# Attention's values for two heads at once in plain fp32, v kept in fp32, key norms spread by transposes

## The chip, the cores and the metric

The kernel runs on one core of one Trainium2 chip. The metric is the device time of one execution in microseconds (us), the median of several runs. In the profile PE is TensorE (products), PEld its weight loads, DVE VectorE, ACT ScalarE, POOL GpSimd, and SP the engine that issues most DMAs.

## What is computed

One layer of a hybrid decoder, for a new prompt of 1024 tokens and for 64 sample tokens (8 sequences of 8) that continue from caches. The width is 1024.

```python
h = rmsnorm(x); proj = h @ w_in                    # 1024 -> 3328
o_rw = rwkv7(proj[:, :1024])                       # 4 heads of 64, keys normed per head
o_cv = short_conv(proj[:, 1024:1792])              # gated convolution, 3 taps
q, k, v = proj[:, 1792:]                           # 8 heads of 64
q, k = rmsnorm(q), rmsnorm(k)                      # per head
z = (q @ k.T) / 8 + bias                           # stick-breaking attention
beta, keep = sigmoid(z), sigmoid(-z)               # masked: keys before the query
wts = beta * (product of keep over later keys)
o_sb = wts @ v
x = x + concat(o_rw, o_cv, o_sb) @ w_out
x = x + relu(rmsnorm(x) @ w_up)**2 @ w_down        # 4096 wide
x = x + sigmoid(rmsnorm(x) @ w_ple_gate) * (p @ w_ple_proj)
```

In the RWKV part the keys kk = k * k_k are divided by their norm over each head's 64 channels. The new k and v rows are outputs too. Everything is fp32.

## The kernel before

**Precision.** Most products are made of fp32r operands: an fp32 value is split into a high part (a copy to fp32r, on ACT) and a low part (the difference, on DVE or POOL), and a product is the sum of high by high, low by high and high by low, three fp32r products into one PSUM bank. Smaller products of the recurrence, the decode step and the transposes are plain fp32.

**Order.** The kernel is traced as one program in which the stages follow each other; a planner then simulates the engines and writes out the order of each engine and of each DMA queue, from what is ready and what was traced first. So products of later stages stand between those of earlier ones wherever they are ready. A few places fix the order by hand (`issue_after`, `high_priority`, `keep_in_program_order`). `run` steps several generators in turn. Tiles come from pools with a fixed number of buffers; a new tile waits until the last use of the buffer that it takes.

**Key norms (L400 to L434).** For each of two groups j of 128 channels, `rw_tile` projects kx, L410 sums the squares per head with tokens on the partitions, and L412/L413 make 1 / sqrt (`rk`, 128 tokens x 9 blocks x 2 heads). The norms must then be spread over the 64 channels and turned so that channels lie on the partitions: L422 writes the broadcast high part in fp32r, L425 the low part, and L431 multiplies each of 9 blocks of both parts with an fp32r identity (18 products for each j). L433 multiplies kx with the result. After it come the matrices of the recurrence (`wkv_products`), and for j = 1 `wkv_base`, a chain of small DVE steps, whose result goes out to DRAM and comes back for the recurrence.

**Projections (L890 to L918).** v is projected first, then q and k, in blocks of 128 tokens; `project` copies a block from PSUM to `nat`. For v (n == 2) it writes the output and splits the block (L866 on ACT, L867 on POOL) into `spl`, which holds for four heads 64 high and 64 low columns; L868 writes it to `v_s` in DRAM, 16 writes. `stack` transposes q and k, splits them and writes `stk_s`.

**Attention (L923 to L1016).** `attention` is traced twice: for the first 512 queries (q0, q1 = 0, 2), with the convolution stepping beside it (`run(*[conv] * 5, *[att] * 4)`), and for the last 512 (2, 4), ahead of the MLP. A unit is a head h and a block qb of 256 queries, head by head; 16 units in each call. `prep` loads a head's stacked keys and queries and its values `vs` (high and low columns side by side). `weights` makes, for each half of the block (128 queries i), the scores by L961 and L962, the sigmoids on ACT, the masks on POOL (L968), the scan over later keys (L970) and the product with beta (L972) on DVE, or on POOL for odd i in the second call. `values` follows AHEAD = 2 units later. It takes the keys 256 at a time: four transposes (L990) of 128 x 128 weights into one of two banks, the high part by ACT and the low part by DVE (`split`, L60 and L61), then for each 128 keys a product of `vs` with the high part (L1000) and one with the low part (L1001), both 128 columns wide since `vs` holds high and low, into one output bank (`obank`, a single bank). L1003 copies one half of the output, L1004 adds the other, and L1005 writes 64 rows to `mix_s` from SP.

**Convolution (L1023 to L1082).** Three groups of 256 columns of w_in; the last (L1068) is loaded as one set of weights and used for j = 0 and 1.

Of the kernel before, what the change touches and what calls it, by code (L numbers as in the profile page):

```python
# [21 lines left out]
F32 = mybir.dt.float32  # L22
F32R = mybir.dt.float32r
# [8 lines left out]
NP = 1024  # L32
# [3 lines left out]
T = NP + NS  # L36
# [5 lines left out]
NA = 15  # L42
AA = 2
CA = (5, 4)
AB_ = 2


@with_exitstack
def hybrid_step(ctx: ExitStack, tc: tile.TileContext, I, O):
# [6 lines left out]
    def f(t):  # L56
        return t.bitcast(F32)

    def split(dst_hi, dst_lo, src):
        S.copy(dst_hi, src)  # L60
        V.tensor_sub(dst_lo, src, f(dst_hi))  # L61

# [28 lines left out]
    stk_s = dram.tile([2, 8, 2, 64, NP], F32, name="stk_s")  # L91
    v_s = dram.tile([8, 8, 128, 128], F32, name="v_s")
    new_s = [dram.tile([NS, 512], F32, name=f"new{n}") for n in range(3)]
# [27 lines left out]
    make_identity(nc, ident)  # L121
    ident_r = consts.tile([128, 128], F32R)
    G.tensor_copy(ident_r, ident)
    bones = consts.tile([128, 128], F32)
# [275 lines left out]
    for j in range(2):  # L400
# [12 lines left out]
        V.reciprocal(rk, rk)  # L413
        rbs = []
        for a in range(2):
            rb = pe_tile("rb", F32R)
            rbs.append((rb, rp.tile([128, 2, 64], F32R, name=f"rb8{a}")))
            for d, i0, i1 in ((rb[:, :1024], 0, 8), (rbs[a][1].rearrange("p s d -> p (s d)"), 8, 9)):
                d = d.rearrange("p (i s d) -> p i s d", i=i1 - i0, s=2)
                src = rk[:, i0:i1, :, None].to_broadcast([128, i1 - i0, 2, 64])  # L420
                if a == 0:
                    V.tensor_copy(d, src)  # L422
                else:
                    h = rbs[0][0][:, :1024] if i0 == 0 else rbs[0][1].rearrange("p s d -> p (s d)")
                    V.tensor_sub(d, src, f(h).rearrange("p (i s d) -> p i s d", i=i1 - i0, s=2))  # L425
        for t0, n in CH:
            ps = tr()
            for t in range(t0, t0 + n, 128):
                r = min(128, T - t)
                for a in range(2):  # L430
                    PE.matmul(ps[:, t - t0:t - t0 + r], rbs[a][0][:, t:t + 128] if t < NP else rbs[a][1].rearrange("p s d -> p (s d)"),  # L431
                              ident_r[:, 128 - r:], start=a == 0, stop=a == 1)
            V.scalar_tensor_tensor(kn[:, t0:t0 + n], kx[:, t0:t0 + n], P1("k_k", j), ps[:, :n], op0=ALU.mult,  # L433
                                   op1=ALU.mult)  # L434
# [414 lines left out]
    def project(n, ps, i0, nat, i):  # L849

        t0 = 128 * (i0 + i)
        flat = nat[:, i]
        S.copy(flat, ps)
        if n < 2:
            normed(flat, ps)
        to = outs[n][0][0, 0].rearrange("t h d -> t (h d)") if n else None
        if n == 1:
            SP.dma_start(to[t0:t0 + 128, :], gained(n, flat))
        if n == 2 and i:
            SP.dma_start(to[t0 - 128:t0 + 128, :].rearrange("(i p) c -> p i c", p=128), nat)  # L860
        if n == 2:
            src = flat.rearrange("p (h d) -> p h d", h=8)
            for hf in range(2):
                hs = slice(4 * hf, 4 * hf + 4)
                spl = sbp.tile([128, 4, 128], F32R, name="spl", tag="st", bufs=4)
                S.copy(spl[:, :, 0:64], src[:, hs])  # L866
                G.tensor_sub(spl[:, :, 64:128], src[:, hs], f(spl[:, :, 0:64]))  # L867
                SP.dma_start(v_s[hs, i0 + i].rearrange("h p e -> p h e"), f(spl))  # L868

    def stack(hf, n, i0, nat):  # L870
# [12 lines left out]
        for e in range(2):  # L883
            for s in range(2):
                (S, SP)[e].dma_start(stk_s[n, 4 * hf + s:4 * hf + 4:2, e, :, i0 * 128:i0 * 128 + 256]
                                     .rearrange("r d t -> d r t"),
                                     f(hl[e])[64 * s:64 * s + 64])

# [34 lines left out]
    def attention(ap, q0, q1, zbank, wbank, obank, AHEAD):  # L923
# [5 lines left out]

        heads = {}  # L930

        def prep(h):

            stk = []
            for name, n, r0 in (("k", 1, 0), ("q", 0, 256 * q0), ("x", 0, 256 * q0)):
                r = slice(r0, 256 * q1)
                o = ap.tile([128, 256 * q1 - r0], F32R, name=f"stk_{name}", bufs=2)
                if name == "x":
                    for e in range(2):
                        SP.dma_start(f(o)[64 * e:64 * e + 64], stk_s[n, h, 1 - e, :, r])  # L940
                else:
                    SP.dma_start(f(o), stk_s[n, h, :, :, r].rearrange("e d t -> (e d) t"))
# [5 lines left out]
        wts = {}  # L948

        def weights(h, qb):  # L950
            kk, qa, qx, _ = heads[h]
            for i in (2 * qb, 2 * qb + 1):
                L = 128 * (i + 1)
                q = slice(i * 128 - 256 * q0, i * 128 + 128 - 256 * q0)
                beta = ap.tile([128, 256 * q1], F32, name="beta", bufs=2 * AHEAD + 2)
                keep = ap.tile([128, 256 * q1 + 1], F32, name="keep", bufs=3 if q0 else 2)
# [15 lines left out]
                (G if i % 2 and q0 else V).tensor_mul(beta[:, 0:L], beta[:, 0:L], keep[:, 1:L + 1])  # L972
                wts[h, i] = beta

        def values(h, qb):
            vs = heads[h][3]
            pr, s = divmod(h, 2)
            d = slice(64 * s, 64 * s + 64)
            po = obank()
            last_kt = 2 * qb + 1  # L980
            for g in range(qb + 1):
                pw = wbank()
                wh = ap.tile([128, 2, 256], F32R, name="wth", bufs=2)
                wl = ap.tile([128, 2, 256], F32R, name="wtl", bufs=2)
                p3 = pw.rearrange("p (k q) -> p k q", k=2)
                for e in range(2):
                    kt = 2 * g + e
                    for i in range(2):
                        if 2 * qb + i >= kt:
                            PE.transpose(p3[:, e, i * 128:i * 128 + 128],  # L990
                                         wts[h, 2 * qb + i][:, kt * 128:kt * 128 + 128], ident)
                if g < qb:
                    split(wh, wl, p3)
                else:
                    split(wh[:, 0], wl[:, 0], p3[:, 0])
                    split(wh[:, 1, 128:], wl[:, 1, 128:], p3[:, 1, 128:])
                for e in range(2):
                    kt = 2 * g + e
                    c = slice(128 if kt == last_kt else 0, 256)
                    PE.matmul(po[:, c], vs[:, kt, :], wh[:, e, c], start=kt == 0, stop=False)  # L1000
                    PE.matmul(po[:, c], vs[:, kt, :], wl[:, e, c], start=False, stop=kt == last_kt)  # L1001
            o32 = ap.tile([128, 256], F32, name="o32", bufs=2)
            S.copy(o32[d], po[64 - 64 * s:128 - 64 * s, 0:256])  # L1003
            V.tensor_add(o32[d], po[d, 0:256], o32[d])  # L1004
# [3 lines left out]
        prep(0)  # L1008
        for n in range(len(units) + AHEAD):
            if n < len(units):  # L1010
                if n % (q1 - q0) == 0 and units[n][0] < 7:
                    prep(units[n][0] + 1)
                weights(*units[n])
            if n >= AHEAD:
                values(*units[n - AHEAD])
            yield  # L1016
# [6 lines left out]
    def convolution():  # L1023
        cst = cv.tile([16, 256], F32, name="cst")
        SP.dma_start(cst, I["state_conv"][0].rearrange("b i c -> (b i) c"))
        CV0 = 1024
# [11 lines left out]
        for j in range(2):  # L1038
# [17 lines left out]
            for i in range(2):  # L1056
# [10 lines left out]
                                   op0=ALU.mult, op1=ALU.add)  # L1067
        w = W.load(w_in[:, CV0:CV0 + 256])  # L1068
        for j in range(2):
            y = cc[j]  # L1070
            for t0, n in CH:
                ps = gemm_cv()
                gemm_t(ps, w, j, hT, t0, n)
                np_ = min(n, NP - t0)
                V.tensor_mul(y[:, t0:t0 + np_], ps[:, :np_], y[:, t0:t0 + np_])
                if np_ < n:
                    y3 = ue[j][:, 0:NS].rearrange("p (b j) -> p b j", j=NJ)
                    V.tensor_mul(y3, ps[:, np_:n].rearrange("p (b j) -> p b j", j=NJ),
                                 y[:, NP + 2:NP + 2 + NB * 10].rearrange("p (b j) -> p b j", j=10)[:, :, 0:NJ])
                yield  # L1080
# [607 lines left out]
```

## Time and profile before

| | us |
|---|---|
| median of 3 runs | 1682.45 (1681.75 to 1683.1) |
| the profiled execution | 1685.16 |
| its span from first to last instruction | 1683.5 |

The profile is one execution. Its page gives the busy time of each engine, the chain of work that ended last, and groups of instructions by line; other views give busy time by stage, each engine's waits by who ended them, and single instructions in order of time. Engines work beside each other, so idle time of one that the others do not wait for costs nothing. The starts of PE's products are good, their ends are modelled: the cost of a product is read from its start to the next start.

The mean granted clock of PE is 0.986 over the span. Stages lie at about these times: key norms 88 to 140 us, projection of v from 165 us, first attention call with the convolution from about 455 us, second call until about 866 us with products of the output projection and the MLP beside it, then the decode step and the rest of the MLP.

### The profile page before, as it was taken

The page shows a single profiled execution, that of the slowest core. Times are in us where ns is not written, and L with a number is a line of the kernel's source. Part 1 is how long each engine was busy: PE and PEld are TensorE (multiplying, and loading weights), DVE is VectorE, ACT ScalarE, POOL GpSimd, SP SyncE. Part 2 cuts the span into 40 slices and gives each one's busy share as a digit, 9 for nine tenths or more (in the row PEclk, how much of TensorE's full clock was granted, in tenths as well). Part 3 has the DMA queues.
Part 4 walks back from the last instruction along what each step waited for, and adds up shares of the span by engine and source line. Part 5 has one row for each costly group of instructions (what it writes and reads, how often), then busy time and mean ns, then how long its engine had stood idle before and what let it go on. Part 6 is the DMA issues. An engine that isn't in the chain of part 4 may idle for free.

```text
span 1683.5 us, 29402 instructions
## 1 busy us (share of the span) xinstructions
PE 1627.7 (97%) x11229; PEld 1435.7 (85%) x11229; DVE 1052.4 (63%) x1822; ACT 791.9 (47%) x1583; POOL 716.8 (43%) x799
## 2 busy tenths in 40 slices
PE   5999999999998999999999999999999999999998
PEld 5999777778897777888887778988999999999898
DVE  5366834455389679878754345277777776768432
ACT  6733235334256467666543444374444444437321
POOL 5221412133255454433435644367555545638210
PEclk8999999999999999999999999999999999999999
DMA  6134575444445453443245556322222232322211
GB/s 206 65 119 138 159 184 135 108 111 120 115 130 175 146 156 105 129 128 106 80 140 167 175 160 213 92 76 89 87 90 89 86 92 88 98 76 88 72 46 41
DMA packets 201470, 196.93 MB, mean 117 GB/s; under 512 B 57969, under 2 KB 161425, under 8 KB 201202
## 3 DMA queue, kind: packets, MB, share of 16 engines
q1 hardware_dynamic: 189330, 173.52, 34.6%
q0 software_dynamic: 5120, 16.78, 3.2%
q10 hardware_dynamic: 6880, 4.75, 1.2%
q8 instruction: 88, 1.44, 0.4%
q14 instruction: 52, 0.43, 0.1%
HBM read 158.03 MB, written 36.98 MB: 116 GB/s over the span
## 4 chain that ended last, share of the span: by engine, by line
PE 49%; DVE 4%; DMA 3%; ACT 1%; issue 1%; POOL 1%; ACTq 0%; DVEq 0%; POOLq 0%; SPq 0%
PE b L1144 11%; PE b L1145 11%; PE b L1146 11%; PE b L1501 3%; PE b L1502 3%; PE b L1503 3%; DMA wr<-in_w_up 1%; PE b L990 1%; PE b L1269 1%; DMA wr<-in_w_down 1%; PE b L1001 1%; PE b L1000 1%; DMA kpg<-in_cache_k,idx 1%; DVE x L1541 1%; PE b L1250 1%
## 5 line engine op out<-in xcount | busy, mean ns | idle before, releaser
L1125 POOL TENSOR_TENSOR wl<-wr,wh 128x512 fp32r<-128x512 f32 x137 | 198.0, 1450 | 207.7 <-ACT wh L1124 190.8
L1541 DVE TENSOR_TENSOR x<-b,x 128x288 f32<-128x288 f32 (+1 forms) x384 | 198.3, 528 | 86.7 <-PE b L1146 85.6
L1124 ACT CAST wh<-wr 128x512 fp32r<-128x512 f32 x233 | 143.8, 622 | 220.6 <-PE b L1145 153.4
L1144 PE MATMUL b<-ah,wh 128*128 128x288 f32 (+1 forms) x612 | 202.2, 331 | 2.5 <-DVE x L1541 1.4
L1146 PE MATMUL b<-ah,wl 128*128 128x288 f32 (+1 forms) x612 | 200.7, 328 | 0.0
L1145 PE MATMUL b<-al,wh 128*128 128x288 f32 (+1 forms) x612 | 200.7, 328 | 0.0
L1144 PE MATMUL b<-nh,wh 128*128 128x512 f32 (+1 forms) x352 | 131.5, 374 | 5.7 <-DVE x L1456 2.1
L1145 PE MATMUL b<-nl,wh 128*128 128x512 f32 (+1 forms) x352 | 130.4, 370 | 0.0
L1146 PE MATMUL b<-nh,wl 128*128 128x512 f32 (+1 forms) x352 | 130.0, 370 | 0.0
L1144 PEld LDWEIGHTS b<-ah,wh 128*128 128x128 f32 x612 | 114.8, 188 | 13.1 <-DVE x L1541 3.9
L1145 PEld LDWEIGHTS b<-al,wh 128*128 128x128 f32 x612 | 115.0, 188 | 8.2 <-issue 0.8
L1146 PEld LDWEIGHTS b<-ah,wl 128*128 128x128 f32 x612 | 114.9, 188 | 8.0
L173 PE MATMUL b<-h_hi,wh 128*128 128x384 f32 (+1 forms) x336 | 114.7, 341 | 1.3 <-ACT xs L353 0.6
L174 PE MATMUL b<-h_lo,wh 128*128 128x384 f32 (+1 forms) x336 | 113.8, 339 | 0.0
L175 PE MATMUL b<-h_hi,wl 128*128 128x384 f32 (+1 forms) x336 | 112.3, 334 | 0.0
L970 DVE TENSOR_TENSOR_SCAN keep<-keep,onesq 128x128 f32<-128x128 f32 (+3 forms) x64 | 98.5, 1539 | 16.7 <-POOL keep L968 16.1
L161 POOL TENSOR_TENSOR wl<-wr,wh 128x512 fp32r<-128x512 f32 x40 | 54.9, 1387 | 103.4 <-ACT wh L158 102.5
L1125 POOL TENSOR_TENSOR wsl<-s,wsh 128x512 fp32r<-128x512 f32 x60 | 79.0, 1337 | 35.9 <-ACT wsh L1124 29.0
L1125 DVE TENSOR_TENSOR wl<-wr,wh 128x512 fp32r<-128x512 f32 x96 | 75.5, 789 | 25.3 <-ACT wh L1124 21.8
L1144 PEld LDWEIGHTS b<-nh,wh 128*128 128x128 f32 x352 | 66.4, 189 | 17.4 <-DVE x L1456 2.5
L908 PE MATMUL b<-wl,h_hi 128*128 128x512 f32 x192 | 77.7, 405 | 1.8 <-DVE wl L161 1.8
L908 PE MATMUL b<-wh,h_hi 128*128 128x512 f32 x192 | 78.5, 411 | 0.0
(471 smaller groups left out, 4655.2 us busy)
## 6 DMA issues: line engine op xcount, KB each, us to landing
wr<-in_w_up SPq DMA_DIRECT2D x64, 512.0 KB
wr<-in_w_down SPq DMA_DIRECT2D x64, 512.0 KB
wr<-in_w_in SPq DMA_DIRECT2D x26, 512.0 KB
wr<-in_w_out SPq DMA_DIRECT2D x16, 512.0 KB
xt<-in_x_prompt SPq DMA_DIRECT2D x8, 512.0 KB
v_s<-spl SPq DMA_DIRECT2D x16, 256.0 KB
stk_s<-sth ACTq DMA_DIRECT2D x32, 128.0 KB
stk_s<-stl SPq DMA_DIRECT2D x32, 128.0 KB
```

What stands on the lines that cost most here:

```text
L161: sub[k0 // step % 2].tensor_sub(lo, raw[:, c:c + 512], f(hi))
L173: PE.matmul(ps[:, :n], wh[k][:, c], a, start=(k == 0), stop=False)
L174: PE.matmul(ps[:, :n], wh[k][:, c], b, start=False, stop=False)
L175: PE.matmul(ps[:, :n], wl[k][:, c], a, start=False, stop=(k == nk - 1))
L908: last = PE.matmul(ps[i], x[:, t0:t0 + 128], wt, start=start, stop=stop)
L970: V.tensor_tensor_scan(keep[:, 0:L][:, ::-1], keep[:, 0:L][:, ::-1], onesq[:, 0:1].to_broadcast([128, L]), 1.0, op0=ALU.mult, op1=ALU.mult)
L1124: S.copy(h3, src)
L1125: (sub or G).tensor_sub(l3, src, f(h3))
L1144: PE.matmul(ps[:, :n], w(0, k, m), a, start=(k == 0), stop=False)
L1145: PE.matmul(ps[:, :n], w(0, k, m), b, start=False, stop=False)
L1146: PE.matmul(ps[:, :n], w(1, k, m), a, start=False, stop=(k == nk - 1))
L1541: V.tensor_add(p.x[:, m, t0:t0 + n], ps[:, :n], p.x[:, m, t0:t0 + n])
```

## The change

- `values` takes a pair of heads. For every 128 keys both heads' weights are transposed into one bank (`p3`, heads by queries), one ACT copy brings them to SBUF in fp32 (`wt`), and two plain fp32 products follow, one for each head, with 64 columns of `vs` each, into the upper and the lower 64 partitions of the output bank. There is no split and no second product. One ACT copy takes both heads' output, and the DMA to `mix_s` is issued from ACT.
- The values are called when the second head of a pair has its weights. AHEAD is 1 in both calls. `beta` has its own buffers for even and odd i, 3 + AHEAD of each (before, 2 * AHEAD + 2 for both), those of even i 128 columns shorter.
- `v_s` holds v in fp32, by token block, written from `nat` with four DMAs; `vs` is loaded once for a pair, with one buffer in the second call and two in the first.
- The key norms are broadcast once in fp32 (`rb`, `rb8`) and turned by nine plain transposes for each j. `ident_r` goes.
- The last convolution weights are loaded as two sets of 128 columns, the second after the products of j = 0.

```diff
-AA = 2
+AA = 1
-AB_ = 2
+AB_ = 1
...
-        rbs = []
-        for a in range(2):
-            rb = pe_tile("rb", F32R)
...
+        rb = pe_tile("rb")
+        rb8 = rp.tile([128, 2, 64], F32, name="rb8")
+        for d, i0, i1 in ((rb[:, :1024], 0, 8), (rb8.rearrange("p s d -> p (s d)"), 8, 9)):
+            V.tensor_copy(d.rearrange("p (i s d) -> p i s d", i=i1 - i0, s=2),
+                          rk[:, i0:i1, :, None].to_broadcast([128, i1 - i0, 2, 64]))
         for t0, n in CH:
             ps = tr()
-            for t in range(t0, t0 + n, 128):
-                r = min(128, T - t)
-                for a in range(2):
-                    PE.matmul(ps[:, t - t0:t - t0 + r], rbs[a][0][:, t:t + 128] if t < NP else ...,
-                              ident_r[:, 128 - r:], start=a == 0, stop=a == 1)
+            for t in range(t0, min(t0 + n, NP), 128):
+                PE.transpose(ps[:, t - t0:t - t0 + 128], rb[:, t:t + 128], ident)
+            if t0 + n == T:
+                PE.transpose(ps[:, n - 128:n], rb8.rearrange("p s d -> p (s d)"), ident)
...
         if n == 2 and i:
             SP.dma_start(to[t0 - 128:t0 + 128, :].rearrange("(i p) c -> p i c", p=128), nat)
-        if n == 2:
-            src = flat.rearrange("p (h d) -> p h d", h=8)
-            for hf in range(2):
-                hs = slice(4 * hf, 4 * hf + 4)
-                spl = sbp.tile([128, 4, 128], F32R, name="spl", tag="st", bufs=4)
-                S.copy(spl[:, :, 0:64], src[:, hs])
-                G.tensor_sub(spl[:, :, 64:128], src[:, hs], f(spl[:, :, 0:64]))
-                SP.dma_start(v_s[hs, i0 + i].rearrange("h p e -> p h e"), f(spl))
+            SP.dma_start(v_s[i0:i0 + 2].rearrange("i p c -> p i c"), nat)
...
-            vs = ap.tile([128, 2 * q1, 128], F32R, name="vs", bufs=2)
-            SP.dma_start(f(vs), v_s[h, 0:2 * q1].rearrange("i p e -> p i e"))
-            heads[h] = stk + [vs]
+            heads[h] = stk
+            if s == 0:
+                vals[pr] = ap.tile([128, 2 * q1, 128], F32, name="vs", bufs=1 if q0 else 2)
+                SP.dma_start(vals[pr], v_s[0:2 * q1, :, 128 * pr:128 * pr + 128].rearrange("i p c -> p i c"))
...
-                beta = ap.tile([128, 256 * q1], F32, name="beta", bufs=2 * AHEAD + 2)
+                beta = ap.tile([128, 256 * q1 - 128 + 128 * (i % 2)], F32, name=f"beta{i % 2}", bufs=3 + AHEAD)
...
+        def values(pr, qb, wts):
+            vs = vals[pr]
             po = obank()
             last_kt = 2 * qb + 1
+            for kt in range(last_kt + 1):
+                p3 = wbank().rearrange("p (s q) -> p s q", s=2)
+                i0 = kt == last_kt
+                c = slice(128 * i0, 256)
+                for s in range(2):
+                    for i in range(i0, 2):
+                        PE.transpose(p3[:, s, i * 128:i * 128 + 128], wts[s][i][:, kt * 128:kt * 128 + 128], ident)
+                w = ap.tile([128, 2, 256], F32, name="wt", bufs=3)
+                S.copy(w[:, :, c], p3[:, :, c])
+                for s in range(2):
+                    PE.matmul(po[hs(s), c], vs[:, kt, hs(s)], w[:, s, c], start=kt == 0, stop=kt == last_kt)
             o32 = ap.tile([128, 256], F32, name="o32", bufs=2)
-            S.copy(o32[d], po[64 - 64 * s:128 - 64 * s, 0:256])
-            V.tensor_add(o32[d], po[d, 0:256], o32[d])
-            SP.dma_start(mix_s[4 + pr, d, qb * 256:qb * 256 + 256], o32[d])
+            S.copy(o32, po[:, 0:256])
+            S.dma_start(mix_s[4 + pr, :, qb * 256:qb * 256 + 256], o32)
...
+            h, qb = units[n - AHEAD] if n >= AHEAD else (0, 0)
+            if h % 2:
+                values(h // 2, qb, [made.pop((h - 1 + s, qb)) for s in range(2)])
...
-        w = W.load(w_in[:, CV0:CV0 + 256])
         for j in range(2):
+            w = W.load(w_in[:, CV0 + 128 * j:CV0 + 128 * j + 128], ncol=128)
...
-                gemm_t(ps, w, j, hT, t0, n)
+                gemm_t(ps, w, 0, hT, t0, n)
```

More of the change, by code (lines that the diff above doesn't have):

```diff
@@ L91, in hybrid_step @@
     stk_s = dram.tile([2, 8, 2, 64, NP], F32, name="stk_s")
-    v_s = dram.tile([8, 8, 128, 128], F32, name="v_s")
+    v_s = dram.tile([8, 128, 512], F32, name="v_s")
     new_s = [dram.tile([NS, 512], F32, name=f"new{n}") for n in range(3)]
@@ L121, in hybrid_step @@
     make_identity(nc, ident)
-    ident_r = consts.tile([128, 128], F32R)
-    G.tensor_copy(ident_r, ident)
     bones = consts.tile([128, 128], F32)
@@ L928, in attention @@
         V.tensor_scalar(bias[:, 1], bias[:, 0], -1.0, None, op0=ALU.mult)
-        heads = {}
+        heads, vals = {}, {}
         def prep(h):
+            pr, s = divmod(h, 2)
             stk = []
             for name, n, r0 in (("k", 1, 0), ("q", 0, 256 * q0), ("x", 0, 256 * q0)):
-                r = slice(r0, 256 * q1)
+                src = stk_s[n, h, :, :, r0:256 * q1]
                 o = ap.tile([128, 256 * q1 - r0], F32R, name=f"stk_{name}", bufs=2)
@@ L939, in prep, with hs @@
                     for e in range(2):
-                        SP.dma_start(f(o)[64 * e:64 * e + 64], stk_s[n, h, 1 - e, :, r])
+                        SP.dma_start(f(o)[64 * e:64 * e + 64], src[1 - e])
                 else:
-                    SP.dma_start(f(o), stk_s[n, h, :, :, r].rearrange("e d t -> (e d) t"))
+                    SP.dma_start(f(o), src.rearrange("e d t -> (e d) t"))
                 stk.append(o)
-            vs = ap.tile([128, 2 * q1, 128], F32R, name="vs", bufs=2)
-            SP.dma_start(f(vs), v_s[h, 0:2 * q1].rearrange("i p e -> p i e"))
-            heads[h] = stk + [vs]
-        wts = {}
+            heads[h] = stk
+            if s == 0:
+                vals[pr] = ap.tile([128, 2 * q1, 128], F32, name="vs", bufs=1 if q0 else 2)
+                SP.dma_start(vals[pr], v_s[0:2 * q1, :, 128 * pr:128 * pr + 128].rearrange("i p c -> p i c"))
+        def hs(s):
+            return slice(64 * s, 64 * s + 64)
         def weights(h, qb):
-            kk, qa, qx, _ = heads[h]
+            kk, qa, qx = heads[h]
+            wts = []
             for i in (2 * qb, 2 * qb + 1):
@@ L972, in weights @@
                 (G if i % 2 and q0 else V).tensor_mul(beta[:, 0:L], beta[:, 0:L], keep[:, 1:L + 1])
[L973 to L978, printed above, removed]
+                wts.append(beta)
+            return wts
+        def values(pr, qb, wts):
+            vs = vals[pr]
             po = obank()
             last_kt = 2 * qb + 1
[L981 to L1001, printed above, removed]
@@ L1010, in attention @@
             if n < len(units):
[L1011 to L1015, printed above, removed]
+                h, qb = units[n]
+                if qb == q0 and h < 7:
+                    prep(h + 1)
+                made[h, qb] = weights(h, qb)
+            h, qb = units[n - AHEAD] if n >= AHEAD else (0, 0)
+            if h % 2:
+                values(h // 2, qb, [made.pop((h - 1 + s, qb)) for s in range(2)])
```

17 lines of the change are left out of this document (2 added, 15 removed).

## The prediction

> **What bounds the kernel now.** I read the page's engine totals first, then the busy time by stage, then the waits of TensorE (PE), then single instructions in order of time.
>
> ```profile
> span 1683.5 us, 29402 instructions
> PE 1627.7 (97%) x11229; PEld 1435.7 (85%) x11229; DVE 1052.4 (63%) x1822; ACT 791.9 (47%) x1583; POOL 716.8 (43%) x799
> ```
>
> PE is busy 97% of the span, so what counts is PE's own time and the few places where it waits. The change sits in three stages: key norms (88 to 140 us), the projection of v (165 to 250) and attention (440 to 870). Each row gives length, then busy time and instructions of PE, PEld (weight loads), DVE, ACT and POOL, then granted clock, DMA share and GB/s.
>
> ```profile
> core 0: us, PE busy (x) PEld busy (x) DVE busy (x) ACT busy (x) POOL busy (x), PEclk, DMA share, GB/s
> 165.00:250.00 85.00, 80.63 (x438) 63.40 (x436) 54.55 (x123) 29.94 (x62) 25.14 (x33) 0.96 0.64 179
> 440.00:700.00 260.00, 240.74 (x1483) 202.61 (x1482) 203.99 (x321) 151.50 (x314) 122.02 (x203) 0.95 0.48 142
> 700.00:870.00 170.00, 170.00 (x915) 145.70 (x914) 130.12 (x178) 101.22 (x200) 66.12 (x86) 1.00 0.36 107
> ```
>
> Attention has two faces. After 700 us PE is never idle and runs at clock 1.00: products of the MLP fill every hole, so anything added to PE there is paid in full. Before 700 us PE is idle 260 - 240.74 = 19.3 us, and the mean clock of 0.95 loses up to 0.05 x 260 = 13 us more: 32.3 us in all. DVE is busy 78% of that stretch. PE's waits in attention (total, times, longest) say for whom:
>
> ```profile
> PE b L1000 <- DVE o L1004: 5.5, 2, 4.0
> PE b L1144 <- DVE x L1456: 2.1, 1, 2.1
> ...
> PE b L961 <- DMA stk_q<-stk_s: 1.8, 1, 1.8
> ...
> PE b L1144 <- DVE r L1466: 1.6, 1, 1.6
> PE b L1000 <- ACT wth L60: 1.4, 1, 1.4
> PE b L1144 <- DVE x L1541: 1.1, 2, 0.9
> PE b L1144 <- ACT rb L1407: 1.1, 1, 1.1
> PE b L990 <- DVE beta L972: 0.9, 1, 0.9
> PE b L1001 <- DVE wtl L61: 0.6, 2, 0.4
> ```
>
> The rows that name DVE and ACT sum to 14.3 us, 11.8 of them DVE's. The largest is the single output bank: the next values product waits until L1004 has read it.
>
> **The values products on PE.** Before, a step of 128 keys takes per head two fp32r products (weights hi and lo) of 256 columns. One core's TensorE order; columns are start, modelled duration, line and shape:
>
> ```profile
> 700.88 0.28 PE L1000 MATMUL b<-wth,vs 128*128 128x256 f32 x1
> ...
> 701.83 0.27 PE L990 MATMUL b<-ident,beta 128*128 128x128 f32 x1
> ...
> 483.44 0.22 PE L1000 MATMUL b<-wth,vs 128*128 128x128 f32 x1
> 483.50 0.27 PE L962 MATMUL b<-stk_k,stk_x 128*128 128x128 f32 x1
> ```
>
> Between 700.88 and 701.83 stand eight of them: 0.95 / 8 = 0.119 us from start to start. For a pair of heads a step costs 4 x 0.119 = 0.48 us; the last step of a block, with 128 columns, 4 x 0.06 = 0.24.
>
> After, the step is two plain fp32 products, 64 columns of the array each. The trace has this form in the sample chunk's L765, with 512 columns; an fp32 product shows as two records there. Ahead of it one row of the chain that ended last, for a transpose: 0.90 / 8 = 0.11 us.
>
> ```profile
> 842.14 0.90 PE b L990 x8
> ```
>
> ```profile
> 511.77 0.39 PE L990 MATMUL b<-ident,beta 128*128 128x128 f32 x2
> 512.09 1.08 PE L765 MATMUL b<-um,AB 128*64 128x512 f32 x4
> 513.10 0.33 PE L990 MATMUL b<-ident,beta 128*128 128x128 f32 x1
> ...
> 546.32 1.07 PE L765 MATMUL b<-um,AB 128*64 128x512 f32 x2
> 547.32 0.49 PE L1144 MATMUL b<-mh,wh 128*128 128x512 f32 x1
> 547.65 0.39 PE L1145 MATMUL b<-ml,wh 128*128 128x512 f32 x1
> 547.88 0.39 PE L1146 MATMUL b<-mh,wl 128*128 128x512 f32 x1
> ...
> 117.32 0.34 PE L173 MATMUL b<-h_hi,wh 128*128 128x384 f32 x1
> 117.49 1.99 PE L475 MATMUL b<-xs,bones 128*128 128x384 f32 x6
> 119.08 0.58 PE L174 MATMUL b<-h_lo,wh 128*128 128x384 f32 x1
> 119.50 0.34 PE L175 MATMUL b<-h_hi,wl 128*128 128x384 f32 x1
> ```
>
> Two heads' products (x4) take 513.10 - 512.09 = 1.01 us, one alone (x2) 1.00: the two halves of the array work side by side, the second head is free. Per column and record fp32 costs 0.85 ns: L475's six records have 4 x 384 + 2 x 320 = 2176 columns, from 117.49 to 119.50 less the 0.17 us of one such product as L173. So 512 columns in two records are 0.87 us and L765 has 0.14 us beside its columns. The way in costs 0.10 (two transposes at 0.11 from 511.77 end at 511.99, L765 starts at 512.09), the way out 0.05 to 0.10 (547.32 to 547.65 is 0.33, the next such step 0.23). I take 0.32 us a group for coming and going. A step of 256 columns then is 2 x 256 x 0.85 ns + 0.32 = 0.755 us, 0.28 over before; a last step 0.218 + 0.32 = 0.54, 0.30 over. A pair of heads has 2 + 4 + 6 + 8 = 20 steps in its four blocks, 80 in all, 16 of them last: 64 x 0.28 + 16 x 0.30 = +22.7 us if every group stands alone. The eight at 700.88 are two groups in one row; an estimate from that order is that a fifth of the groups has a neighbour and saves 16 x 0.32 = 5.1. I take +17.6 us; ends +10 (half the groups have a neighbour, 40 x 0.32 saved) and +32 (rival C with every group alone). The transposes stay, 288 of them.
>
> Here a rule speaks against the change. By the Trainium skill, TensorEngine Tiling, section Key Properties, changing the tiling mode, unlike changing the tile, drains the engine. The trace agrees (0.10 us in, about as much out). The same page's section Theoretical Speedup promises up to twice the speed for 64 columns; on that alone the 80 steps would cost their bare columns, 64 x 0.435 + 16 x 0.218 = 31.3 us against 34.6 before, a gain of 3 us; with the drain the sum is the +22.7 above.
>
> Where they fall: records with wth or its values, by stage (PE, PEld, DVE, ACT), and the outputs o below (DVE, ACT).
>
> ```profile
> 440.00:700.00 260.00, 20.13 (x76) 14.52 (x76) 26.69 (x60) 24.35 (x60) 0.95 0.48 142
> 700.00:870.00 170.00, 21.65 (x84) 15.83 (x84) 27.36 (x53) 23.96 (x52) 1.00 0.36 107
> ...
> 440.00:700.00 260.00, 8.36 (x20) 7.34 (x20) 0.95 0.48 142
> ```
>
> 76 of 160 lie before 700 us: +8.4 us there, +9.2 after it, where nothing hides it.
>
> **What DVE and ACT lose.** All low halves (L61) and the adds (L1004) go: before 700 us DVE loses 26.69 + 8.36 = 35 of 204 us. One ACT copy of 256 columns replaces copy plus add, so the output bank opens one engine sooner, and the weights' bank opens after the copy and not after DVE's subtraction. Of the 14.3 us of waits I take two thirds, 9.5: L1004's 5.5 is gone with its instruction, the others only get a shorter queue. Next late is ACT's copy. Of the 13 us of lost clock I take half, 6.5, since it lies around those waits. Ends: 0 and -32.3. Sum -16.0. After 700 us the relief of 27 us on DVE buys nothing, PE has no wait there.
>
> **Key norms.**
>
> ```profile
> 93.63 1.76 PE L431 MATMUL b<-ident_r,rb 128*128 128x128 f32 x15
> 95.53 0.44 PE L173 MATMUL b<-h_hi,wh 128*128 128x384 f32 x1
> L425 DVE TENSOR_TENSOR rb<-rk,rb x4: 1217/1268/1322, 89.7 to 137.5; 128x1024 fp32r<-128x1024 f32 x2, 128x128 fp32r<-128x128 f32 x2
> ```
>
> 36 products at 0.11 us (x15 in 1.76) become 18 transposes at the same 0.11: -2.0 us of PE. DVE's four subtractions of 1.27 us go, two of them (2.5 us) on the path of j = 1 to the long chain of wkv_base on DVE. In 165 to 250 us PE idles 4.4 us, for that chain's DVE work and the loads behind it; starting it 2.5 us earlier may save up to that. I take -1.5 (0 to -4).
>
> **Edits at nothing.**
>
> ```profile
> L866 ACT CAST spl<-nat x16: 400/406/411, 170.9 to 204.7; 128x256 fp32r<-128x256 f32 x16
> L867 POOL TENSOR_TENSOR spl<-nat,spl x16: 729/830/982, 171.4 to 206.2; 128x256 fp32r<-128x256 f32 x16
> L885 ACTq DMA_DIRECT2D stk_s<-sth x32: 582/594/1034, 237.4 to 407.8; - x32
> ```
>
> v's split: 6.5 us of ACT and 13 of POOL go beside PE's projections, and 16 issues on SP become 4. None of them is on PE's path: PE is busy 80.63 of 85 us there and the 4.4 were named above. The writes of the output move from SP (32) to ACT's queue (16). An issue there costs 0.59 us by L885, 9.5 us of ACT in 430; behind it stands the next copy of weights, and PE has other products meanwhile. If that cover is gone: +9. Loads of vs are halved; in the second call one buffer remains, so a load waits for the values of the pair before, with the next heads' keys and queries and raw weights behind it on SP. The nearest row is the 1.8 us on stk_q: 0 to 3 x 1.8 = 5; I take 0, since the pair needs it three units later. The last convolution weights come as two loads of 128 columns, the second later: 0, attention fills PE; at worst one more such wait, 1.8. AHEAD 1 with four buffers of each parity holds as many units as the pairing needs: 0, and its worst is a wait like L990's 0.9.
>
> **Sum.** +17.6 - 16.0 - 2.0 - 1.5 = -1.9 us. The profiled run took 1685.16 us (span 1683.5 and 1.7 around it), 2.7 above the median of 1682.45. Against its own time 1683.3, against the median 1680.5 us. A measurement of this kernel tells about 0.2%, 3.4 us, from no change, so my forecast is a balance: no change that can be told.
>
> **Rivals.**
> B, DVE and not PE bounds attention before 700 us. Then all 32.3 us can go and only PE's added 8.4 stays: -23.9 + 9.2 - 2.0 - 1.5 = -18, 1664 us. For: DVE 204 of 260 us, 11.8 of 14.3 us of waits. Against: 35 us is 17% of its work, and the scans and norms remain.
> C, slower: the planner leaves every group alone and sets other work between the two heads' products. A parted head costs its 0.435 + 0.32 = 0.75 us again. With 12 of 80 parted: 22.7 + 9 - 16.0 - 3.5 = +12, 1695. For: L765 itself, x4 once and x2 the other time. It decides once 7 more groups are parted than in my sum (5.3 us / 0.75).
> D, the wait is replaced: the units' chain (sigmoids, POOL's masks, scan) still sets the pace, so only L1004's 5.5 us returns and no clock: 17.6 - 5.5 - 3.5 = +8.6, 1691. For: a unit passes ACT, POOL and DVE one after the other ahead of its transposes, and the change shortens none of those steps. Against: POOL is named in none of PE's waits, and L1004 was the longest. With C as well it would be 1704.
> E, the change does not do what it says, the halves run one after the other: 64 x 0.435 + 16 x 0.218 = +31, 1712. L765 speaks against it.
>
> **Chances.** Balance 0.40 (its own range 1672 to 1688: 0.15 faster, 0.19 within, 0.06 slower), B 0.27, C 0.18, D 0.13, E 0.02. Faster 0.15 + 0.27 = 0.42, same 0.19, slower 0.06 + 0.33 = 0.39. The range from 1662 to 1705 leaves out the far side of B and E.
>
> **What will show it.** Values groups of two heads with starts 0.01 us apart, and 0.7 to 0.8 us from a group's first start to the next other work: else E, or C where one head stands alone. DVE down by about 35 us before 700 us and by 27 or more after it. PE idle of the attention before 700 us down from 19.3 to about 10, clock up to 0.97; still 19: D; near 0: B. Key norms: 18 transposes with no second pass on DVE. Wrong it would be above all by the number of groups that stand alone and by how much of the 32.3 us comes back.

## The result and the profile after

| | us |
|---|---|
| before, median of 4 runs | 1682.1 (1680.56 to 1683.1) |
| after, median of 4 runs | 1672.72 (1670.73 to 1674.71) |
| the profiled execution after | 1674.71, span 1673.0 |

The ratio is 0.9945, 95% interval 0.9928 to 0.9962: 9.4 us less. The forecast was 1680.5 and "a balance". The time lies inside the range and the sign was the likelier one, but the gain was not forecast, and it did not come from attention: that it lies there is more luck than mechanism. One run of the changed kernel (2049 us) and one of attention alone (4930 us) below were far slower than all others and are left out of the ratios; they move a median by 0.1 us.

The page of after, engine totals; line numbers are the changed kernel's:

```profile
span 1673.0 us, 28969 instructions
PE 1625.9 (97%) x11211; PEld 1405.5 (84%) x11211; DVE 977.7 (58%) x1674; ACT 775.4 (46%) x1519; POOL 701.1 (42%) x782
```

DVE lost 75 us and the kernel 9. The same three stages of after, columns as in the prediction:

```profile
165.00:250.00 85.00, 85.00 (x517) 67.87 (x516) 46.07 (x120) 25.45 (x49) 11.67 (x17) 1.00 0.53 149
440.00:700.00 260.00, 245.56 (x1484) 189.77 (x1484) 181.22 (x244) 156.62 (x309) 123.98 (x210) 0.95 0.45 137
700.00:870.00 170.00, 170.00 (x948) 129.67 (x947) 93.02 (x111) 92.80 (x174) 71.48 (x83) 1.00 0.35 108
```

In attention before 700 us PE still idles 260 - 245.56 = 14.4 us (19.3 before) at the same granted clock of 0.95, although DVE has 22.8 us less to do. The stretch that changed is the first row, v's projection: PE busy 85.00 of 85 us where it was 80.63, the clock 1.00 where it was 0.96.

How much that is worth is read from one product that both kernels have, the projections' first product: 192 of them, with the same number of other products between the first and the last in all runs but two (the later split and the split on DVE, below). Before, then after; first and last start:

```profile
L908 PE MATMUL b<-wh,h_hi x192: 387/389/628, 154.4 to 392.4; 128*128 128x512 f32 x192
```

```profile
L886 PE MATMUL b<-wh,h_hi x192: 387/390/631, 150.8 to 380.7; 128*128 128x512 f32 x192
```

The first of the 192 starts 3.6 us earlier, the last 11.7. So all of the gain, and a little more, is there when these products end, before attention begins. It adds up: 2.6 us of key norms on PE, 4.4 us of waits, and an estimate of 0.04 x 85 = 3.4 us of clock make 10.4 of the 11.7.

What held PE in that stretch is the chain of wkv_base on DVE, 46 pairs of small steps. Before, then after:

```profile
L292 DVE TENSOR_TENSOR base_Q<-base_Z,base_X x46: 151/332/1211, 164.7 to 207.1; 128x31 f32<-128x31 f32 x2, 128x60 f32<-128x60 f32 x2, 128x87 f32<-128x87 f32 x2, 128x112 f32<-128x112 f32 x2
L294 DVE TENSOR_TENSOR base_X<-base_X,base_Q x46: 161/343/1224, 164.9 to 207.2; 128x31 f32<-128x31 f32 x2, 128x60 f32<-128x60 f32 x2, 128x87 f32<-128x87 f32 x2, 128x112 f32<-128x112 f32 x2
```

```profile
L286 DVE TENSOR_TENSOR base_Q<-base_Z,base_X x46: 154/287/502, 159.0 to 192.4; 128x31 f32<-128x31 f32 x2, 128x60 f32<-128x60 f32 x2, 128x87 f32<-128x87 f32 x2, 128x112 f32<-128x112 f32 x2
L288 DVE TENSOR_TENSOR base_X<-base_X,base_Q x46: 164/300/1281, 159.3 to 192.6; 128x31 f32<-128x31 f32 x2, 128x60 f32<-128x60 f32 x2, 128x87 f32<-128x87 f32 x2, 128x112 f32<-128x112 f32 x2
```

The three numbers behind x46 are the shortest, the median and the longest step in ns. The chain starts 5.7 us earlier, and its last steps 14.7 earlier. Its 92 steps take 28.6 us in all where they took 37.5, and no instruction of them was changed. The timeline of before says why (start, duration, engine, line):

```profile
202.13 0.81 POOL L867 TENSOR_TENSOR spl<-nat,spl 128x256 fp32r<-128x256 f32 x1 [0.61 <-ACT spl L866]
202.37 0.64 DVE L292 TENSOR_TENSOR base_Q<-base_Z,base_X 16x60 f32<-16x60 f32 x1
202.88 1.46 POOL L520 MEMSET TT<- 128x512 f32 x3
203.04 0.21 DVE L294 TENSOR_TENSOR base_X<-base_X,base_Q 16x60 f32<-16x60 f32 x1
...
204.23 0.19 DVE L292 TENSOR_TENSOR base_Q<-base_Z,base_X 16x39 f32<-16x39 f32 x1
204.31 1.29 POOL L161 TENSOR_TENSOR wl<-wr,wh 128x512 fp32r<-128x512 f32 x1
204.45 1.20 DVE L294 TENSOR_TENSOR base_X<-base_X,base_Q 16x39 f32<-16x39 f32 x1
```

A step of 0.21 us takes 0.64 when it begins during one of POOL's subtractions, and one of 0.19 takes 1.20: both end about when POOL ends (202.94 and 203.01, 205.60 and 205.65). Beside POOL's memset a step keeps its 0.21. The first of the two POOL instructions is v's split (L867); the second, L161, splits weights of the projections and stays in the changed kernel. Of the 92 steps before, 17 take more than 0.65 us. Thirteen of them overlap L867 and no other instruction of POOL with two inputs; the three longest, 1.2 us each, stand beside L161 and L841 (an addition). After, one long step is left (the 1281 ns of L288), beside L827, which is L841 of before; L155, the L161 of before, comes after the shorter chain. By the Trainium skill, SBUF — State Buffer, section Who interferes with whom, a DVE instruction with two inputs in SBUF and a GpSimd one that reads SBUF take one read port as an exclusive lock, and one that only writes does not disturb; the trace agrees, with these numbers.

The issues of SP (columns are start, duration, queue and line) that follow the chain's end, before and then after:

```profile
207.83 0.33 SPq L296 DMA_DIRECT2D t_s<-base_X  x1
...
211.50 0.41 SPq L154 DMA_DIRECT2D wr<-in_w_in  x1
```

```profile
193.16 0.47 SPq L290 DMA_DIRECT2D t_s<-base_X  x1
...
198.88 0.37 SPq L148 DMA_DIRECT2D wr<-in_w_in  x1
```

The write of the chain's result waits in SP's queue, and behind it stand the loads for the recurrence and the raw weights of the next projection. The 4.4 us that PE waits in 165 to 250 us name just those (PE's waits of before):

```profile
PE b L541 <- DMA bk<-bk_s: 2.5, 1, 2.5
PE b L908 <- DVE wl L161: 1.8, 1, 1.8
```

### The profile page after: what moved, and what is told of

The parts are those of the page before. It is cut to its first block, busy times and chain, and to the rows that moved or that the text cites. A ratio compares the mean times of both kernels' runs of the same rounds, so it can differ in the third digit from the quotient of the medians.

```text
span 1673.0 us, 28969 instructions
## 1 busy us (share of the span) xinstructions
PE 1625.9 (97%) x11211; PEld 1405.5 (84%) x11211; DVE 977.7 (58%) x1674; ACT 775.4 (46%) x1519; POOL 701.1 (42%) x782
## 5 line engine op out<-in xcount | busy, mean ns | idle before, releaser
L1117 PEld LDWEIGHTS b<-ah,wh 128*128 128x128 f32 x612 | 114.9, 188 | 15.2 <-DVE x L1514 4.1
L952 DVE TENSOR_TENSOR_SCAN keep<-keep,onesq 128x128 f32<-128x128 f32 (+3 forms) x64 | 94.9, 1483 | 46.3 <-POOL keep L950 45.3
L1098 DVE TENSOR_TENSOR wl<-wr,wh 128x512 fp32r<-128x512 f32 x96 | 78.9, 825 | 27.6 <-ACT wh L1097 27.0
L155 POOL TENSOR_TENSOR wl<-wr,wh 128x512 fp32r<-128x512 f32 x40 | 55.7, 1406 | 64.8 <-ACT wh L152 63.8
L886 PE MATMUL b<-wh,h_lo 128*128 128x512 f32 x192 | 76.1, 397 | 0.0
```

The lines of the kernel that those rows point to most:

```text
L155: sub[k0 // step % 2].tensor_sub(lo, raw[:, c:c + 512], f(hi))
L886: last = PE.matmul(ps[i], x[:, t0:t0 + 128], wt, start=start, stop=stop)
L952: V.tensor_tensor_scan(keep[:, 0:L][:, ::-1], keep[:, 0:L][:, ::-1], onesq[:, 0:1].to_broadcast([128, L]), 1.0, op0=ALU.mult, op1=ALU.mult)
L1098: (sub or G).tensor_sub(l3, src, f(h3))
L1117: PE.matmul(ps[:, :n], w(0, k, m), a, start=(k == 0), stop=False)
```

## The experiments

Twelve runs in three groups followed, each group on one chip with before beside it; all ratios are against those runs, and differences in us are between medians on one chip. Theory 1: POOL's share of v's split (L867) slowed the chain, and taking it away is the gain. Theory 2: the key norms alone, by starting the chain earlier. Theory 3: attention.

**The parts one by one.** The key norms' part of the change alone, in before (one fp32 broadcast and 18 transposes in place of the split and 36 products):

> The kernel before with the key norms by transposes and nothing else. Theory 1 (the gain of the change comes from the projection stage: POOL's 16 subtractions of the v split slow the small DVE steps of wkv_base, and the recurrence's inputs and the next weights wait for that chain): the chain still runs beside POOL, 42 us long, and only starts 5 to 6 us earlier; PE gains 2 to 3 us in the key norms and part of its 4.4 us wait: 1682 - 5 = about 1677, and L292 and L294 stay at about 37 us busy. Theory 2 (the key norms alone give the whole early gain by starting the chain earlier): 1682 - 11 = 1671. Theory 3 (the gain comes from attention): 1679 to 1682.

Only POOL's subtraction taken out of before (an ACT copy stands there, so the low parts of v are left out; the 16 writes to `v_s` stay):

```diff
-                G.tensor_sub(spl[:, :, 64:128], src[:, hs], f(spl[:, :, 0:64]))
+                S.copy(spl[:, :, 64:128], src[:, hs])
```

> The kernel before with the low half of v's split written by an ACT copy of v instead of POOL's subtraction (so the low parts of v are left out as such: v's own value stands there), everything else as before, the 16 writes to v_s too. Theory 1: the DVE chain of wkv_base shrinks from 42 to about 34 us, its small steps from 37 to about 29 us busy, PE's waits at 206 to 216 us go with the lost clock around them: 1682 - 7 = about 1675. Theory 2: no change, 1680 to 1683, chain 42 us. If the 16 writes on SP were the cause: no change either.

The changed kernel with the split's work put back, into tiles that nobody reads:

```diff
             SP.dma_start(v_s[i0:i0 + 2].rearrange("i p c -> p i c"), nat)
+        if n == 2:
+            for hf in range(2):
+                ...
+                S.copy(spl[:, :, 0:64], src[:, hs])
+                G.tensor_sub(spl[:, :, 64:128], src[:, hs], f(spl[:, :, 0:64]))
```

> The kernel after with v's split put back as work whose result is not used: ACT's 16 copies and POOL's 16 subtractions into spl, no DMA of them. Theory 1: the chain is 42 us again but begins 5 us earlier than before, ending at about 202 us, so PE loses part of what it gained: 1672.7 + 3 to 6 = about 1677. Theory 2 (key norms): 1672 to 1674. Theory 3 (attention): 1672 to 1674.

And that kernel with the old key norms as well, so that attention's change is left alone:

> The kernel after with the key norms of before and v's split work put back (ACT and POOL, result not used, no DMA of it): what is left of the change is attention, the four writes of v in fp32, the loads and the convolution weights. Theory 1: attention's gain and loss nearly cancel, 1681 to 1686 (by PE's lag between the two profiles +2 us in attention and decode). Theory 3: about 1673, as after.

Measured (before 1690.07 us on this chip): key norms 1683.92, 0.9961 (0.9948 to 0.9974); the split off POOL 1680.88, 0.9944 (0.9931 to 0.9956); after with the split work 1683.69, 0.9953 (0.9937 to 0.9968); attention alone 1688.2, 0.9984 (0.9972 to 0.9995). The stage 165 to 250 us of the four, in this order:

```profile
165.00:250.00 85.00, 79.40 (x454) 63.59 (x454) 51.74 (x116) 28.52 (x59) 25.33 (x33) 0.96 0.61 166
```

```profile
165.00:250.00 85.00, 85.00 (x498) 67.86 (x497) 51.04 (x135) 34.67 (x78) 12.61 (x17) 1.00 0.68 191
```

```profile
165.00:250.00 85.00, 81.44 (x476) 64.99 (x475) 51.02 (x119) 28.34 (x59) 24.42 (x32) 0.98 0.52 145
```

```profile
165.00:250.00 85.00, 76.72 (x417) 61.49 (x415) 53.58 (x122) 27.69 (x58) 24.64 (x33) 0.96 0.53 154
```

PE is full where POOL has 12.6 us to do, and in none of these kernels where it has 24 or 25. One of the chain's two lines in the second kernel, whose instructions on DVE are those of before:

```profile
L292 DVE TENSOR_TENSOR base_Q<-base_Z,base_X x46: 149/288/494, 165.5 to 198.6; 128x31 f32<-128x31 f32 x2, 128x60 f32<-128x60 f32 x2, 128x87 f32<-128x87 f32 x2, 128x112 f32<-128x112 f32 x2
```

The median step is back at 288 ns and the chain ends 8.5 us earlier although it starts 0.8 later; all 92 steps take 28.4 us. With POOL's work put back into after, they take 35.1 us again and the last starts at 199.9. So theory 1 holds for the chain and for this stretch. Theory 2 is right as far as the start: with the key norms alone the chain starts 4.3 us earlier (160.4), but its steps stay long and PE still waits. Theory 3 does not carry the gain: attention alone gained 1.9 us.

The time of the whole kernel follows less closely. The ratio of after with the split work, 0.9953, cannot be told from the changed kernel's 0.9945 (on another chip), where theory 1 had it 3 to 6 us slower, although its last projection product of that kind starts 6.1 us later (386.8 against 380.7). In the order of the four kernels, that product starts 2.1, 7.3, 5.6 and -2.1 us earlier than in before's profile, and the whole gained 6.2, 9.2, 6.4 and 1.9 us: what makes the difference of these two rows, up to about 4 us, stays open.

**Do the gains add, and what is attention worth beside them?** Key norms and the split off POOL together, in before:

> Before, with the key norms of the changed kernel and with the low half of v's split replaced by a second ACT copy (low parts of v are left out); attention as before. Theory 1: the early wait can only go once, so the two gains (0.39% and 0.56% when alone) do not add: 0.994, what the key norms take off PE (2.6 us) on top of the 9.4 at most, -9 to -12 us. If the gains add, because they come from different places: -16 us (0.9905). Set against the changed kernel it says what attention's change is worth: its own ratio of 0.9984 alone says -2.7 us, so this kernel would lie 3 us above the changed one if the parts add; if attention is worth nothing beside the others, both lie together; if it costs the 1.6 us and more of the prediction, this one is the faster.

The changed kernel on the same chip:

> The changed kernel as it is, as the measure for the other three beside it. Theory 1 (the gain is that of the stretch from 165 to 207 us, where POOL's share of v's split no longer slows wkv_base): 0.9945 of before again, and PE busy 85 of 85 us from 165 to 250. If the gain had been one chip's or one run's, the ratio would lie at 0.998 or above.

Measured (before 1681.78): 1667.67, 0.9911 (0.9898 to 0.9925), for the two parts with before's attention; 1672.6, 0.9944 (0.9931 to 0.9956), for the changed kernel. The sum of the single gains was 15.3 us, this is 14.1: they add more than I expected. And the kernel with before's attention is 4.9 us faster than the changed one: beside the two early parts, attention's change, with the loads, writes and weights that go with it, costs time.

**Attention's two terms.** DVE's relief undone but for the adds of the output, everything else as changed:

```diff
                 S.copy(w[:, :, c], p3[:, :, c])
+                for s in range(2):
+                    wl = ap.tile([128, 256], mybir.dt.bfloat16, name="wtl", bufs=1)
+                    V.tensor_sub(wl[:, c], p3[:, s, c], w[:, s, c])
```

> The changed kernel, but DVE subtracts the copied weights from the transposed ones again (as L61 did), in two instructions of 256 columns for each step, into a tile that nobody reads; the bank opens only after it. Everything else as in the changed kernel. Theory of the prediction, DVE's relief before 700 us is worth 16 us: this kernel is 10 to 16 us slower than the changed one, its idle PE from 440 to 700 us back at 19 us or more. Rival (D of the prediction), the units' chain of sigmoids, masks and scan sets the pace and the relief is worth little: 0 to +4 us.

1676.63 us, 0.9966 (0.9954 to 0.9979): 4.0 us above the changed kernel. Its stage before 700 us, and then that of the changed kernel beside it:

```profile
440.00:700.00 260.00, 241.96 (x1466) 187.28 (x1467) 204.81 (x323) 152.42 (x296) 127.57 (x203) 0.98 0.46 138
```

```profile
440.00:700.00 260.00, 247.84 (x1512) 191.48 (x1512) 183.94 (x247) 161.83 (x315) 129.32 (x215) 0.97 0.46 139
```

21 us of DVE work more cost 5.9 us of PE's idle time, no clock, and 4 us in the end. The rival's size was right, at its upper end, as far as this run goes: the adds of L1004 and their wait for the output bank are not in it, and its order parts some pairs of heads (the values products take 41.9 us between their starts and what follows, against 40.0 in the changed kernel beside it).

The coming and going of the values products, halved: both steps of 256 keys wait for the second copy, so that 8 records stand together.

```diff
-            for kt in range(last_kt + 1):
-                ...                                 # transposes, copy, two products
+            for g in range(qb + 1):
+                ...                                 # transposes and copies of kt = 2g, 2g + 1
+                for kt, c, w in step:
+                    for s in range(2):
+                        p = PE.matmul(po[hs(s), c], vs[:, kt, hs(s)], w[:, s, c], ...)
+                        tc.add_manual_dep(p.ins, made_w.ins.name, ...)
```

> The changed kernel with the values products of two steps of 128 keys issued together: 40 clusters of 8 records where the changed kernel has 58 (36 of 4 records, 22 of 8). Theory A, each coming and going between the two shapes of the array costs PE time: 18 clusters fewer at 0.15 us (2 x 0.583 - 1.015 in the changed kernel's trace) is -2.7 us by the trace, at the 0.32 us of the prediction -5.8 us; the part after 700 us counts in full. Theory B, it costs nothing that matters: no change. Theory C, the pair needs both banks of transposed weights at once, so transposes wait for copies and PE waits more: +3 us or more.

1673.47 us, 0.9951 (0.9936 to 0.9966), against 1672.6 for the changed kernel: no gain seen, as theory B has it; the intervals overlap, so that A's 2.7 us are unlikely and not ruled out. Over all groups the values products take 4.7 us less of PE (37.5 us between their starts and what follows, and 0.093 us ahead of each of 40 groups; 40.5 and 58 groups in the changed kernel's first profile), an estimate. Of this 4.4 us lie before 700 us, where PE has idle time anyway, and 0.4 after it, where 22 of 34 steps were together already.

**Where to put the split.** If POOL is in the chain's way, the split can stay and move. Before's attention, the key norms of the change, v to DRAM in fp32, and back during the projection of k:

```diff
+    def split_v(i):
+        vr = sbp.tile([128, 512], F32, name="vr", tag="kg", bufs=2)
+        SP.dma_start(vr, v32_s[i])
+        ...                                 # S.copy, G.tensor_sub and DMA to v_s as before
...
+            if n == 1:
+                for i in range(2):
+                    split_v(i0 + i)
```

> Before with the key norms of the changed kernel, and v's split moved behind the chain of wkv_base: v goes to DRAM in fp32 as in the changed kernel and comes back during the projection of k, where ACT and POOL split it as before (8 loads and 4 writes more, nothing left out). Attention as before. Theory 1 with attention's change as a loss: 0.991 of before as the kernel with key norms and the split off POOL, so about 5 us faster than the changed kernel. If that kernel's gain came from the low parts that it left out, or if the split, wherever it stands, costs its POOL time: 0.994 to 0.996, no faster than the changed kernel.

The subtraction on DVE at its old place:

```diff
-                G.tensor_sub(spl[:, :, 64:128], src[:, hs], f(spl[:, :, 0:64]))
+                V.tensor_sub(spl[:, :, 64:128], src[:, hs], f(spl[:, :, 0:64]))
```

> Before with the key norms of the changed kernel and v's low half subtracted on DVE where POOL did it, at the same place. Nothing left out. It tells apart how POOL's work slows the chain of wkv_base: if it is POOL's tensor operations beside DVE's that stretch the chain's steps, the steps are short again (28 us of DVE in all, not 37) and only the 16 subtractions themselves (0.3 to 0.5 us each, 5 to 8 us, most of them in gaps of the chain or ahead of it) come on top: 0.991 to 0.994. If it is any work on the same data, for example the transfers of spl, the steps stay at 35 to 37 us and the time at 0.996 as with the key norms alone, or worse.

Beside them attention alone and the changed kernel once more:

> The changed kernel with the key norms and the split work of before back in it, once more, beside the other three on one chip: attention's change alone. The first time it was 0.9984 (0.9972 to 0.9995) of before, -2.7 us, while the changed kernel stands 4.9 us behind the kernel with before's attention, key norms and the split off POOL. If attention costs 5 us wherever it stands: 1.003. If its price depends on when attention starts, or on the state of the early stretch: 0.998 to 0.9995 again.

> The changed kernel as the measure beside the other three on this chip: 0.9944 of before again; the kernel with the later split is expected 5 us below it, the kernel with DVE's split 0 to 5 us below it, and attention alone 9 to 14 us above it.

Measured (before 1683.58): later split 1668.2, 0.9903 (0.9887 to 0.9918); split on DVE 1675.34, 0.9952 (0.9937 to 0.9967); attention alone 1684.09, 1.0000 (0.9989 to 1.0010); the changed kernel 1671.08, 0.9925 (0.9910 to 0.9940). The split where it comes later, then on DVE with the chain's two lines:

```profile
165.00:250.00 85.00, 85.00 (x505) 67.89 (x503) 47.09 (x122) 24.90 (x48) 11.66 (x17) 1.00 0.54 149
L865 POOL TENSOR_TENSOR spl<-vr,spl x16: 725/732/744, 299.9 to 395.0; 128x256 fp32r<-128x256 f32 x16
```

```profile
L859 DVE TENSOR_TENSOR spl<-nat,spl x16: 411/420/1359, 165.5 to 202.4; 128x256 fp32r<-128x256 f32 x16
L292 DVE TENSOR_TENSOR base_Q<-base_Z,base_X x46: 151/310/1301, 160.0 to 200.2; 128x31 f32<-128x31 f32 x2, 128x60 f32<-128x60 f32 x2, 128x87 f32<-128x87 f32 x2, 128x112 f32<-128x112 f32 x2
L294 DVE TENSOR_TENSOR base_X<-base_X,base_Q x46: 155/287/495, 160.2 to 200.9; 128x31 f32<-128x31 f32 x2, 128x60 f32<-128x60 f32 x2, 128x87 f32<-128x87 f32 x2, 128x112 f32<-128x112 f32 x2
```

The same 16 subtractions on POOL, 100 us later, cost nothing that shows: the whole early gain stands with v split and attention untouched. On DVE, in the middle of the chain, they lengthen it to 201 us, but its 92 steps take 29.4 us in all (35.7 with POOL's split and the same key norms), and PE is busy 84.28 of 85 us. So it is POOL beside DVE that stretches the steps, not the work itself. The time of that kernel lies between the two ranges that I had given, so it is the steps that decide. It gained 8.2 us where the later split gained 15.4, in an order of its own (the last of the 192 products starts at 358 us, not at 392). It has one wait that no other kernel has for longer than 0.7 us; that it accounts for the difference is likely and not shown:

```profile
584.88 0.80 PE L1136 MATMUL b<-mh,wh 128*128 128x512 f32 x1 [6.36 <-ACT mh L1332]
```

The kernel with the later split is the fastest that computes everything: 15.4 us below before. It is 2.9 us below the changed kernel here. The intervals of the two ratios overlap, but both hold the scatter of before; set against each other, the slowest of its five runs (1669.52) is below the fastest of the changed kernel's six (1669.7). The kernel without the low parts, with the same early stretch and the same attention, stood 4.9 below the changed kernel on the other chip, with intervals that part.

## Why the prediction was right and wrong

**The early part, forecast -3.5, measured -14.1 and -15.4.** The two are the key norms with the split off POOL and with the later split. This is the step that failed, in two sentences of it. "Edits at nothing" put v's split at 0 because "None of them is on PE's path". The work was not on PE's path, but POOL's subtractions stretched DVE's steps, and the chain of wkv_base was on it: the same chain to which I had put down the 4.4 us of waits. And "earlier start of the chain" was bounded by 0 to -4, the 4.4 us of idle PE alone; the clock of 0.96 in the very row that I quoted (3.4 us) was left out of the bound. Both could have been read beforehand: 17 of the chain's 92 steps are longer than 0.65 us at a median of 332 ns, and the timeline shows what stands beside them. The longest step alone would have misled: it does not stand beside v's split, and a step of that length is in the changed kernel too.

**Key norms, -2.0.** 18 transposes, in two rows of nine; the first:

```profile
91.70 1.04 PE L416 MATMUL b<-ident,rb 128*128 128x128 f32 x8
92.57 0.27 PE L418 MATMUL b<-ident,rb 128*128 128x128 f32 x1
```

The next product starts at 92.60, 0.90 us after the first transpose. Both groups take 1.8 us where the 36 products took 4.4, from start to next start: -2.6.

**The values products, +17.6.** Rows of after:

```profile
504.22 0.65 PE L972 MATMUL b<-wt,vs 128*64 128x256 f32 x4
504.80 0.33 PE L968 MATMUL b<-ident,beta 128*128 128x128 f32 x1
...
620.82 1.08 PE L972 MATMUL b<-wt,vs 128*64 128x256 f32 x8
621.84 1.09 PE L968 MATMUL b<-ident,beta 128*128 128x128 f32 x8
```

A group of two heads takes 0.58 us and 0.09 ahead of it, 0.67 where I had 0.755; a double one 1.02. The halves do work side by side (rival E is out). 36 groups stand alone, 44 in 22 doubles, and none is parted (C is out): I had a fifth with a neighbour, it is more than half. Of this term, then, the price of a group and the number of groups that stand alone were both too high. In all 40.5 + 58 x 0.093 = 45.9 us against 34.6 before, an estimate of +11.3; my lower end was +10. The 0.093 are the 0.203 us from the last transpose's start to a group's first start (median of the 15 groups that stand right behind a transpose) less 0.11 for the transpose itself. By the Trainium skill, TensorEngine Tiling (Array Packing), section Key Properties, a change of the tiling mode drains the engine; the 0.09 us agree.

**DVE's relief, -16.0.** Undoing it, but for the adds of the output, cost 4.0 us. I had taken two thirds of the waits that name DVE and ACT and half of the lost clock; the profile after shows what came next instead:

```profile
PE b L943 <- DMA stk_q<-stk_s: 5.0, 2, 4.8
PE b L968 <- DVE beta L954: 3.8, 2, 2.8
PE b L1030 <- DVE ue L1025: 1.8, 1, 1.8
```

L1000's 5.5 us are gone and a load of queries at the start of the second call, which I had put at 0 (0 to 5), is late by 4.8. The two other profiles of the changed kernel show the same rows, with 2.5 and 4.3 us for the queries and 3.7 each for beta. That was rival D in attention, PE idle 14.4 us and not 10; B would have needed the idle time near 0. The other two profiles say the same of the idle time (12.2 and 15.2 us), and those with before's attention and the early parts have 17.2 and 17.8. So 4 to 5 us of idle time came back where I had 9.5. Of the clock nothing can be told: it is 0.95, 0.97 and 0.98 in three profiles of the changed kernel, and 0.95 to 0.97 in those with before's attention, so the 6.5 us that I had for it are not shown.

**Attention's sum, +1.6.** Measured -1.9 and +0.5 alone, +4.9 and +2.9 beside the early parts. That it is about right is luck: both terms were too large, by 6 and by up to 12 us, and their errors cancel. The measured +11.3 and -4.0 leave +7.3. The rest may be PE's idle time, which took part of the products, and the waits for the output bank; I did not measure these apart. Alone it also loses 2.1 us early (the projections' last such product at 394.5 us, behind a wait of 8.3 us for bk), so that it wins more in its own stage than its total shows. Why it gains there alone, and costs time beside the early parts, stays open. So does most of the key norms' own 6.2 us: the last of their early products starts only 2.1 us earlier (390.3 against 392.4).

**A slip in the rivals.** D with C sums to 22.7 + 9 - 5.5 - 3.5 = +22.7, 1705 us and not 1704.

**DVE's busy time:** forecast 35 us less before 700 us and 27 after; 22.8 and 37.1, since attention's last values product starts at 829 us and not at 866, so that less of it lies after 700.

## What to carry to other kernels

Work on an engine that nobody waits for is free only if it does not slow an engine that somebody waits for: before an edit is put at nothing, look at the steps of the critical chain that it runs beside, count those that are far longer than others of their shape, and see what stands beside each. When a wait is named, its bound is the idle time and the lost clock around it, not the idle time alone. Here, moving such work 100 us later was worth as much as removing it, and left nothing of the computation out.

## What was not expected of the hardware

A DVE step of 0.19 us took 1.20 us beside a POOL subtraction of 1.29, ending with it, and the 92 steps of the chain, 28.6 us without v's split on POOL, took 37.5 beside it. Beside POOL's memset they kept their length. The early stretch repeats within a microsecond on different chips (the 192 products start from 150.8 to 380.7, 150.6 to 380.6 and 151.5 to 381.4 us in the changed kernel's three profiles), while medians of before differ by 8 us between them (1681.78 and 1690.07): so each time is compared with that of before on its own chip.
